# An encoder layer's weight split: row scales moved from the weights to the activations, four row tiles to an instruction

## The chip, the cores and the metric

One core of a Trainium2 chip runs the whole layer. The metric is the device time of the kernel in microseconds (us), the median of several runs. Engines are named as in the profile: PE (TensorE; PEld its weight loads), DVE (VectorE), ACT (ScalarE), POOL (GpSimd), SP (SyncE, which here issues the DMA transfers).

## The reference

One layer over 256 tokens of width 2048, all in fp32. Every sub-layer is wrapped in two root-mean-square norms, one before (with a gain per feature) and one after:

```
def _rmsnorm(x, g):
    return x * rsqrt(mean(x * x, -1) + EPS) * g
def _swiglu(u, w_gate, w_up, w_down):
    return (silu(u @ w_gate) * (u @ w_up)) @ w_down

h = h + 0.5 * _rmsnorm(_swiglu(_rmsnorm(h, ffn1_pre_g), ...), ffn1_post_g)   # D_FF = 5632
h = h + _rmsnorm(_mixer(_rmsnorm(h, mix_pre_g), w_qkv, na_rpb, out_g, w_o), mix_post_g)
h = h + 0.5 * _rmsnorm(_swiglu(_rmsnorm(h, ffn2_pre_g), ...), ffn2_post_g)
g = sigmoid(_rmsnorm(h, ple_pre_g) @ w_ple_gate)
h = h + _rmsnorm(g * (p @ w_ple_proj), ple_post_g)
```

The mixer has 16 heads of 128: 4 with neighbourhood attention, 12 with a mixture of dilated windows. Their outputs are normed per head, multiplied by `out_g` and projected by `w_o`. Five of the gains (the three `pre_g` of the FFNs and the mixer, `ple_pre_g`, `out_g`) multiply the rows of a weight matrix if one wishes: u * g @ w is the same as u @ (g * w).

## The kernel before

**Splitting.** Matmuls run on a rounded fp32 type (`F32R`). To keep precision each factor is split into a high part (a copy into that type) and a low part (the rest), and every product is three matmuls: high by high, low activation by high weight, high activation by low weight. Tokens make two tiles `t` of 128; `NB` = 512 output columns make one block, whose two accumulators (one per token tile) are PSUM tiles of `ps_acc` (4 buffers).

**The weights** stream from HBM in fp32, each used once per token tile. `load_pairs` (L61) fetches up to four row tiles of 128x512 by one DMA on SP (`raw`, 3 buffers) and splits them into pairs: `wh` and `wl` hold two row tiles each and have 7 buffers, 14 row tiles. Where the product has a gain (`g`), each row tile is one ACTIVATE on ACT with the gain as per-partition scale (L79) and one scalar_tensor_tensor on DVE, raw * g - wh (L80). The products without one (down, the embedding's projection) copy and subtract a pair at a time (L74, L75).

**A product** (`product`, L89) goes through its rows in groups of `SUPER` = 8 row tiles: load and split the group, then for both token tiles and all 8 row tiles the three matmuls L114, L115, L116, 48 in all. The very first gate product takes groups of 1, 1, 2, 2, ..., the very first up groups of 4 (L240 to L242), as x and h arrive (`load_x`, L176; `load_h`, L185). Between groups it runs the jobs that were put off (`later`); `mid` is called three row tiles before the end of the last group (L108).

**The activations** are split as they are made, in `transposed_split` (L146): four PE transposes of a 128x512 block into a PSUM tile `tr` (`ps_tr`, 2 buffers), ACT's copy to the high part (L152), DVE's subtract to the low part (L153). It is called for the hidden blocks of the FFNs (`hid`), for the heads' outputs (`on`, L431), and at the end of a stage in `residual` (L198): h += f * r on DVE (L210), then the transposed split of h into `u_h`, `u_l`, for two token tiles and four blocks. The factors r of the norms come from sums of squares on ACT (L144), a reduction on DVE (L137) and two small POOL instructions (L138, L139); they are applied to the products when these are read from PSUM.

**Stages.** First FFN; q, k, v and attention in four rounds of four heads; `w_o` (`mo`); second FFN; the embedding's projection (`pp`) and gate (`pg`). An FFN takes its 11 hidden blocks in groups of 4, 4 and 3 (`FF_GROUPS`): for each block gate and up, then for the group down, whose rows are these blocks' columns. The last hidden block of a group is thus turned just when its down product begins. At the end of a stage `residual` makes the next stage's operand: three transitions, first FFN to q, mixer (`mo`) to second FFN's gate, second FFN to `pg` (with `pp` in between).

**Order.** Each engine runs its instructions in one program order, which the framework's scheduler makes from the code; buffers are handed on by semaphores. An instruction whose operand is late holds up all that stand behind it on its engine.

Of the kernel before, what the change touches and what calls it, by code (L numbers as in the profile page):

```python
# [8 lines left out]
F32 = mybir.dt.float32  # L9
# [19 lines left out]
MID = 3  # L29
BIG = 3.0e38  # L30
# [3 lines left out]
def encoder_layer(ctx: ExitStack, tc: tile.TileContext, a: dict, out: bass.AP):  # L34
# [26 lines left out]
    def load_pairs(w, r0, nk, c0, g):  # L61


        pairs = []
        for k0 in range(0, nk, 4):
            n = min(4, nk - k0)
            raw = wpool.tile([P, 4, NB], F32, name="raw", bufs=3)
            rows_ = w[r0 + k0 * P : r0 + (k0 + n) * P, c0 : c0 + NB]
            raw_loads.append(nc.sync.dma_start(raw[:, :n], rows_.rearrange("(k p) n -> p k n", p=P)))
            for j in range(0, n, 2):  # L70
                wh = wpool.tile([P, 2, NB], F32R, name="wh", bufs=7)
                wl = wpool.tile([P, 2, NB], F32R, name="wl", bufs=7)
                if g is None:
                    nc.scalar.copy(wh, raw[:, j : j + 2])  # L74
                    nc.vector.tensor_tensor(wl, raw[:, j : j + 2], wh.bitcast(F32), op=ALU.subtract)  # L75
                else:
                    for i in range(min(2, n - j)):
                        k = r0 // P + k0 + j + i
                        nc.scalar.activation(wh[:, i], raw[:, j + i], AF.Copy, scale=g[:, k : k + 1])  # L79
                        nc.vector.scalar_tensor_tensor(  # L80
                            wl[:, i], raw[:, j + i], g[:, k : k + 1], wh[:, i].bitcast(F32),
                            op0=ALU.mult, op1=ALU.subtract,
                        )
                pairs.append((wh, wl))
        return pairs
# [3 lines left out]
    def product(  # L89
        acc, lhs, w, r0, c0, g=None, first=True, last=True, steps=None, ahead=None, mid=None, jobs=True  # L90
    ):

        nk = len(lhs)
        s0 = 0  # L100
        for n in steps or [nk % SUPER] * (nk % SUPER > 0) + [SUPER] * (nk // SUPER):
            if ahead is not None:
                ahead(s0)
            pairs = load_pairs(w, r0 + s0 * P, n, c0, g)
            for t in range(NT):
                tok = slice(t * P, (t + 1) * P)
                for k in range(n):
                    if mid is not None and t == NT - 1 and s0 + n == nk and k == n - MID:  # L108
                        mid()
                    wh, wl = pairs[k // 2]  # L110
# [3 lines left out]
                    nc.tensor.matmul(acc[t], xh[:, tok], wh[:, k % 2], start=lead, stop=False)  # L114
                    nc.tensor.matmul(acc[t], xl[:, tok], wh[:, k % 2], start=False, stop=False)  # L115
                    nc.tensor.matmul(acc[t], xh[:, tok], wl[:, k % 2], start=False, stop=tail)  # L116
# [29 lines left out]
    def transposed_split(x, hi, lo, t):  # L146

        tr = ps_tr.tile([P, KB, P], F32, name="tr", tag="tr")
        for k in range(KB):
            nc.tensor.transpose(tr[:, k], x[:, k * P : (k + 1) * P], ident)  # L150
        tok = slice(t * P, (t + 1) * P)
        nc.scalar.copy(hi[:, :, tok], tr)  # L152
        nc.vector.tensor_tensor(lo[:, :, tok], tr, hi[:, :, tok].bitcast(F32), op=ALU.subtract)  # L153
# [22 lines left out]
    def load_x(k):  # L176
        if k % 2:
            return
        hi, lo = (u[:, k % KB : k % KB + 2] for u in x_blocks[k // KB])
        xb = work.tile([P, 2, S], F32, name="xb", tag="hg")  # L180
        nc.sync.dma_start(xb, xT[:, k : k + 2])
        nc.scalar.copy(hi, xb)
        nc.vector.tensor_tensor(lo, xb, hi.bitcast(F32), op=ALU.subtract)
# [14 lines left out]
    def residual(fg, ssf, scale, blocks, rs):  # L198

        blocks += [new_split(acts, "u", D // NB) for _ in range(D // NB)]
        r = []
        for b0 in range(0, D // NB, 2):
            for t in range(NT):
                if b0 == 0:
                    r.append(rsqrt_mean(ssf[t], D, scale))
                for b in range(b0, b0 + 2):
                    cols = slice(b * NB, (b + 1) * NB)
                    nc.vector.scalar_tensor_tensor(  # L210
                        h[:, t, cols], fg[:, t, cols], r[t], h[:, t, cols], op0=ALU.mult, op1=ALU.add
                    )
# [7 lines left out]
    def swiglu(pool, f, ssf, res, blocks, rs, g_pre, w_gate, w_up, w_down, g_post):  # L220
        lhs = rows(blocks)
        f0 = 0
        for gi, ng in enumerate(FF_GROUPS):
            hid = []
            for nb in range(f0, f0 + ng):
# [69 lines left out]
    with ExitStack() as att:  # L295
# [84 lines left out]
        def attend(qT, kT, v, bias, o_split):  # L380

            for t in range(NT):
# [48 lines left out]
                later.append(lambda on=on, t=t: transposed_split(on, *o_split, t))  # L431
# [3 lines left out]
        for g in range(4):  # L435
# [5 lines left out]
            product(acc, lhs, a["w_qkv"], 0, c[0], g=row_g[:, 1])  # L441
            qT = heads_transposed(acc, rq, g > 0, "qT")
            acc = accs("k")
            product(acc, lhs, a["w_qkv"], 0, c[1], g=row_g[:, 1])
            kT = heads_transposed(acc, rs, g > 0, "kT")
            acc = accs("v")
            product(acc, lhs, a["w_qkv"], 0, c[2], g=row_g[:, 1])
# [8 lines left out]
            attend(qT, kT, v, bias, o_split)  # L456
# [7 lines left out]
    res = residual(f, ssf, 1.0, u_blocks, rs)  # L464
# [7 lines left out]
    for b in range(2):  # L472
        acc = accs("mo")
        product(acc, lhs[:early], a["w_o"], 0, b * NB, g=row_g[:, 4], last=False, jobs=b > 0)
        started.append(acc)
    for b in range(D // NB):
# [9 lines left out]
        product(acc, lhs[k0:], a["w_o"], k0 * P, b * NB, g=row_g[:, 4], first=k0 == 0, mid=mid)  # L486
# [9 lines left out]
    with tc.tile_pool(name="ffn2", bufs=2) as pool:  # L496
# [30 lines left out]
    for b in range(D // NB):  # L527
# [3 lines left out]
        product(acc, lhs, a["w_ple_gate"], 0, b * NB, g=row_g[:, 3])  # L531
# [77 lines left out]
```

## Time and profile before

| | us |
|---|---|
| median of 3 runs | 1991.73 (1990.23 to 1991.98) |
| the profiled execution | 1990.87 |
| its span | 1988.8 |
| PE busy in the span | 1969.9 (99%) |
| DVE busy | 1155.9 (58%) |
| ACT busy | 1050.2 (53%) |
| weight loads: 84 to 88 DMAs of 1 MB each for gate, up and down, median time from issue to landing | 5.0 to 5.1 |

The profile is one execution. Its span runs from the first to the last instruction recorded; all starts in the timeline count from the span's start. A row of the groups names line, engine, operation, the tile written and those read, the form, the count, and then busy us, mean ns of one, and the idle time of the engine just before them with what ended it. A row of the timeline begins with start and duration in us; consecutive like instructions are drawn together (x8), and the brackets tell how long the engine stood idle before and what ended that.

### The profile page before, as it was taken

How to read it: one execution, taken by the hardware profiler on the slowest of the kernel's cores; microseconds unless marked ns; L12 is line 12 of the kernel's file. 1: busy time of each engine (PE TensorE's matmuls, PEld its weight loads, DVE VectorE, ACT ScalarE, POOL GpSimd, SP SyncE). 2: the span in 40 equal slices, each digit the busy share in tenths (PEclk: the TensorE clock that was granted, in tenths of full speed). 3: DMA queues.
4: the chain of work that ended last, by engine and by line, in shares of the span. 5: the costliest groups of instructions: out<-in, count | busy, mean ns of one | idle time of the engine just before them, and what ended most of it. 6: DMA issues, size and time to landing. Idle time of an engine off the chain costs nothing.

```text
span 1988.8 us, 23482 instructions
## 1 busy us (share of the span) xinstructions
PE 1969.9 (99%) x8936; PEld 1629.7 (82%) x8936; DVE 1155.9 (58%) x1659; ACT 1050.2 (53%) x1613; POOL 25.4 (1%) x47
## 2 busy tenths in 40 slices
PE   8999999999999999999999999999999999999998
PEld 7888888888888877888888888888888888888886
DVE  5755455655465666566565575654465545565764
ACT  7645455544455455655556564544454534454663
POOL 0000000000000000000000000000000000000000
PEclk9999999999999999999999999999999999999999
DMA  8755555555555557364554555555555555555562
GB/s 302 242 192 187 194 193 189 190 191 188 194 198 183 197 183 224 134 201 138 170 170 168 187 192 200 179 203 175 206 181 200 179 201 184 197 183 203 172 213 102
DMA packets 194561, 377.02 MB, mean 190 GB/s; under 512 B 10768, under 2 KB 13968, under 8 KB 194192
## 3 DMA queue, kind: packets, MB, share of 16 engines
q1 hardware_dynamic: 194448, 375.52, 55.1%
q8 instruction: 70, 1.15, 0.2%
q14 instruction: 43, 0.35, 0.0%
HBM read 373.40 MB, written 2.10 MB: 189 GB/s over the span
## 4 chain that ended last, share of the span: by engine, by line
PE 96%; DMA 1%; DVE 1%; ACT 1%; issue 0%; POOL 0%; SPq 0%; DVEq 0%; POOLq 0%; ACTq 0%
PE down L116 8%; PE down L114 8%; PE down L115 8%; PE up L116 8%; PE up L114 8%; PE up L115 8%; PE gate L116 8%; PE gate L115 8%; PE gate L114 8%; PE tr L150 2%; PE q L116 1%; PE q L115 1%; PE q L114 1%; PE pg L116 1%; PE pg L114 1%; PE k L116 1%
## 5 line engine op out<-in xcount | busy, mean ns | idle before, releaser
L79 ACT ACTIVATE wh<-raw,row_g 128x512 fp32r<-128x512 f32 x1024 | 686.7, 717 | 456.0 <-PE up L115 184.2
L80 DVE SCALAR_TENSOR_TENSOR wl<-raw,row_g,wh 128x512 fp32r<-128x512 f32 x1024 | 708.6, 749 | 335.9 <-ACT wh L79 335.8
L75 DVE TENSOR_TENSOR wl<-raw,wh 128x1024 fp32r<-128x1024 f32 x180 | 220.0, 1224 | 167.5 <-ACT wh L74 153.1
L74 ACT CAST wh<-raw 128x1024 fp32r<-128x1024 f32 x180 | 189.8, 1055 | 213.1 <-PE down L115 168.7
L114 PE MATMUL gate<-wh,u_h 128*128 128x512 f32 x704 | 276.5, 393 | 6.0 <-ACT wh L79 6.0
L116 PE MATMUL gate<-wl,u_h 128*128 128x512 f32 x704 | 275.2, 391 | 0.0
L115 PE MATMUL gate<-wh,u_l 128*128 128x512 f32 x704 | 275.1, 391 | 0.0
L114 PE MATMUL down<-wh,hid_h 128*128 128x512 f32 x704 | 274.5, 390 | 0.0
L116 PE MATMUL down<-wl,hid_h 128*128 128x512 f32 x704 | 274.1, 389 | 0.0
L116 PE MATMUL up<-wl,u_h 128*128 128x512 f32 x704 | 274.0, 389 | 0.1
L114 PE MATMUL up<-wh,u_h 128*128 128x512 f32 x704 | 274.0, 389 | 0.0
L115 PE MATMUL down<-wh,hid_l 128*128 128x512 f32 x704 | 273.9, 389 | 0.0
L115 PE MATMUL up<-wh,u_l 128*128 128x512 f32 x704 | 273.9, 389 | 0.0
L114 PEld LDWEIGHTS gate<-wh,u_h 128*128 128x128 f32 x704 | 132.9, 189 | 32.9 <-ACT wh L79 6.0
L116 PEld LDWEIGHTS gate<-wl,u_h 128*128 128x128 f32 x704 | 132.7, 188 | 27.9 <-DVE wl L80 0.3
L116 PEld LDWEIGHTS up<-wl,u_h 128*128 128x128 f32 x704 | 132.1, 188 | 28.2 <-DVE wl L80 0.5
L115 PEld LDWEIGHTS gate<-wh,u_l 128*128 128x128 f32 x704 | 132.8, 189 | 27.0
L114 PEld LDWEIGHTS up<-wh,u_h 128*128 128x128 f32 x704 | 132.1, 188 | 27.5 <-ACT wh L79 0.3
L115 PEld LDWEIGHTS up<-wh,u_l 128*128 128x128 f32 x704 | 132.1, 188 | 27.4
L115 PEld LDWEIGHTS down<-wh,hid_l 128*128 128x128 f32 x704 | 132.2, 188 | 27.4
L116 PEld LDWEIGHTS down<-wl,hid_h 128*128 128x128 f32 x704 | 132.1, 188 | 27.4
L114 PEld LDWEIGHTS down<-wh,hid_h 128*128 128x128 f32 x704 | 132.2, 188 | 27.0
(122 smaller groups left out, 1813.6 us busy)
## 6 DMA issues: line engine op xcount, KB each, us to landing
raw<-in_ffn_w_up SPq DMA_DIRECT2D x88, 1024.0 KB, 5.1
raw<-in_ffn_w_down SPq DMA_DIRECT2D x88, 1024.0 KB, 5.0
raw<-in_ffn_w_gate SPq DMA_DIRECT2D x84, 1024.0 KB, 5.1
raw<-in_w_qkv SPq DMA_DIRECT2D x48, 1024.0 KB, 5.1
raw<-in_w_o SPq DMA_DIRECT2D x16, 1024.0 KB, 5.0
raw<-in_w_ple_gate SPq DMA_DIRECT2D x16, 1024.0 KB, 5.0
raw<-in_ffn_w_gate SPq DMA_DIRECT2D x7, 512.0 KB, 4.4
xb<-in_xT SPq DMA_DIRECT2D x8, 256.0 KB, 3.2
```

Of the source, the lines that this page charges most:

```text
L74: nc.scalar.copy(wh, raw[:, j : j + 2])
L75: nc.vector.tensor_tensor(wl, raw[:, j : j + 2], wh.bitcast(F32), op=ALU.subtract)
L79: nc.scalar.activation(wh[:, i], raw[:, j + i], AF.Copy, scale=g[:, k : k + 1])
L80: nc.vector.scalar_tensor_tensor(wl[:, i], raw[:, j + i], g[:, k : k + 1], wh[:, i].bitcast(F32), op0=ALU.mult, op1=ALU.subtract,)
L114: nc.tensor.matmul(acc[t], xh[:, tok], wh[:, k % 2], start=lead, stop=False)
L115: nc.tensor.matmul(acc[t], xl[:, tok], wh[:, k % 2], start=False, stop=False)
L116: nc.tensor.matmul(acc[t], xh[:, tok], wl[:, k % 2], start=False, stop=tail)
L150: nc.tensor.transpose(tr[:, k], x[:, k * P : (k + 1) * P], ident)
```

## The change

Weights are no longer scaled. `load_pairs` makes one copy on ACT and one subtract on DVE for all four row tiles of a load (128x2048), into `wh` and `wl` of four row tiles with 3 buffers each (12 row tiles). The gains go into the activations: `transposed_split` gets an optional gain and then multiplies the transposed block by it on DVE (`y_g`, in the work buffers tagged `hg`, of which there are two), between the transposes and ACT's copy; from then on `tr` is free. That is the case for the 24 blocks of the three transitions and the 8 blocks of the heads' outputs; hidden blocks have no gain. `load_x` multiplies each of its 8 blocks the same way (`xg`).

```diff
-    def load_pairs(w, r0, nk, c0, g):
-        pairs = []
-        for k0 in range(0, nk, 4):
-            n = min(4, nk - k0)
-            raw = wpool.tile([P, 4, NB], F32, name="raw", bufs=3)
+    def load_pairs(w, r0, nk, c0):
+        parts = []
+        for k0 in range(0, nk, QUAD):
+            n = min(QUAD, nk - k0)
+            raw = wpool.tile([P, QUAD, NB], F32, name="raw", bufs=3)
...
-            for j in range(0, n, 2):
-                wh = wpool.tile([P, 2, NB], F32R, name="wh", bufs=7)
-                wl = wpool.tile([P, 2, NB], F32R, name="wl", bufs=7)
-                if g is None:
-                    nc.scalar.copy(wh, raw[:, j : j + 2])
-                    nc.vector.tensor_tensor(wl, raw[:, j : j + 2], wh.bitcast(F32), op=ALU.subtract)
-                else:
-                    for i in range(min(2, n - j)):
-                        k = r0 // P + k0 + j + i
-                        nc.scalar.activation(wh[:, i], raw[:, j + i], AF.Copy, scale=g[:, k : k + 1])
-                        nc.vector.scalar_tensor_tensor(
-                            wl[:, i], raw[:, j + i], g[:, k : k + 1], wh[:, i].bitcast(F32),
-                            op0=ALU.mult, op1=ALU.subtract,
-                        )
-                pairs.append((wh, wl))
-        return pairs
+            wh = wpool.tile([P, QUAD, NB], F32R, name="wh", bufs=3)
+            wl = wpool.tile([P, QUAD, NB], F32R, name="wl", bufs=3)
+            nc.scalar.copy(wh[:, :n], raw[:, :n])
+            nc.vector.tensor_tensor(wl[:, :n], raw[:, :n], wh[:, :n].bitcast(F32), op=ALU.subtract)
+            parts += [(wh[:, i], wl[:, i]) for i in range(n)]
+        return parts
...
-    def transposed_split(x, hi, lo, t):
+    def transposed_split(x, hi, lo, t, g=None):
...
+        if g is not None:
+            y = work.tile([P, KB, P], F32, name="y_g", tag="hg")
+            nc.vector.tensor_tensor(y, tr, g.unsqueeze(2).broadcast_to([P, KB, P]), op=ALU.mult)
+            tr = y
         nc.scalar.copy(hi[:, :, tok], tr)
         nc.vector.tensor_tensor(lo[:, :, tok], tr, hi[:, :, tok].bitcast(F32), op=ALU.subtract)
...
-        nc.scalar.copy(hi, xb)
-        nc.vector.tensor_tensor(lo, xb, hi.bitcast(F32), op=ALU.subtract)
+        xg = work.tile([P, 2, S], F32, name="xg", tag="sq")
+        g = row_g[:, 0, k : k + 2]
+        nc.vector.tensor_tensor(xg, xb, g.unsqueeze(2).broadcast_to([P, 2, S]), op=ALU.mult)
+        nc.scalar.copy(hi, xg)
+        nc.vector.tensor_tensor(lo, xg, hi.bitcast(F32), op=ALU.subtract)
...
-                    transposed_split(h[:, t, cols], *blocks[b], t)
+                    transposed_split(h[:, t, cols], *blocks[b], t, g[:, b * KB : (b + 1) * KB])
...
-                later.append(lambda on=on, t=t: transposed_split(on, *o_split, t))
+                later.append(lambda on=on, t=t: transposed_split(on, *o_split, t, g))
```

The calls of `product`, `swiglu`, `residual` and `attend` lose or gain the gain accordingly. The scheduler sets the changed program in another order; a row of the pieces below is the instruction's place on its engine, its line, its operation, the tile written and those read, its form, and how many alike follow. In the changed kernel L73 is the weights' subtract, L145 the multiply `y_g`, L148 the low part of a transposed block, L179 and L181 `xg` and `u_l` of x, L208 the residual's h, L467 the mixer's and L267 and L264 the FFN's f.

DVE at the program's start, before:

```order
1 L183 TENSOR_TENSOR u_l<-xb,u_h 128x512
2 L80 SCALAR_TENSOR_TENSOR wl<-raw,row_g,wh 128x512 x2
3 L183 TENSOR_TENSOR u_l<-xb,u_h 128x512
4 L80 SCALAR_TENSOR_TENSOR wl<-raw,row_g,wh 128x512 x2
5 L183 TENSOR_TENSOR u_l<-xb,u_h 128x512
```

and now:

```order
1 L179 TENSOR_TENSOR xg<-xb,row_g 128x512 x2
2 L181 TENSOR_TENSOR u_l<-xg,u_h 128x512
3 L73 TENSOR_TENSOR wl<-raw,wh 128x512 x2
4 L181 TENSOR_TENSOR u_l<-xg,u_h 128x512
5 L73 TENSOR_TENSOR wl<-raw,wh 128x1024
6 L179 TENSOR_TENSOR xg<-xb,row_g 128x512 x2
```

The gains of the first and the second x block stand ahead of the first block's low part.

DVE where the mixer ends and the second FFN's gate begins (`mo` are the mixer's last accumulators, `ssf` sums for the norm), before:

```order
392 L210 SCALAR_TENSOR_TENSOR h<-f,r,h 128x512 x4
393 L80 SCALAR_TENSOR_TENSOR wl<-raw,row_g,wh 128x512
394 L153 TENSOR_TENSOR u_l<-tr,u_h 128x4x128 x2
395 L80 SCALAR_TENSOR_TENSOR wl<-raw,row_g,wh 128x512 x2
396 L469 TENSOR_TENSOR f<-mo_8710,g_post 128x512
397 L137 TENSOR_REDUCE m<-ssf 128x1
398 L80 SCALAR_TENSOR_TENSOR wl<-raw,row_g,wh 128x512
399 L210 SCALAR_TENSOR_TENSOR h<-f,r,h 128x512 x4
400 L153 TENSOR_TENSOR u_l<-tr,u_h 128x4x128 x2
```

and now:

```order
395 L208 SCALAR_TENSOR_TENSOR h<-f,r,h 128x512 x4
396 L145 TENSOR_TENSOR y_g<-tr,row_g 128x512 x2
397 L73 TENSOR_TENSOR wl<-raw,wh 128x2048
398 L148 TENSOR_TENSOR u_l<-y_g,u_h 128x4x128 x2
399 L467 TENSOR_TENSOR f<-mo_7416,g_post 128x512
400 L127 TENSOR_REDUCE m<-ssf 128x1
401 L73 TENSOR_TENSOR wl<-raw,wh 128x2048
402 L208 SCALAR_TENSOR_TENSOR h<-f,r,h 128x512 x3
403 L145 TENSOR_TENSOR y_g<-tr,row_g 128x512 x2
404 L208 SCALAR_TENSOR_TENSOR h<-f,r,h 128x512
405 L148 TENSOR_TENSOR u_l<-y_g,u_h 128x4x128 x2
```

Between h and the first `u_l` one weight piece of a row tile has become two `y_g` and a piece of four row tiles; ahead of the second token tile's h it is again a piece of four for a piece of one.

DVE where the second FFN ends and the embedding's gate begins, from the second token tile's h on, before:

```order
563 L210 SCALAR_TENSOR_TENSOR h<-f,r,h 128x512 x4
564 L80 SCALAR_TENSOR_TENSOR wl<-raw,row_g,wh 128x512 x5
565 L137 TENSOR_REDUCE m<-ssh 128x1
566 L153 TENSOR_TENSOR u_l<-tr,u_h 128x4x128 x2
567 L137 TENSOR_REDUCE m<-ssh 128x1
568 L80 SCALAR_TENSOR_TENSOR wl<-raw,row_g,wh 128x512
569 L153 TENSOR_TENSOR u_l<-tr,u_h 128x4x128
```

and now:

```order
563 L208 SCALAR_TENSOR_TENSOR h<-f,r,h 128x512 x3
564 L73 TENSOR_TENSOR wl<-raw,wh 128x1024
565 L208 SCALAR_TENSOR_TENSOR h<-f,r,h 128x512
566 L73 TENSOR_TENSOR wl<-raw,wh 128x2048
567 L145 TENSOR_TENSOR y_g<-tr,row_g 128x512 x2
568 L73 TENSOR_TENSOR wl<-raw,wh 128x2048
569 L148 TENSOR_TENSOR u_l<-y_g,u_h 128x4x128 x2
570 L145 TENSOR_TENSOR y_g<-tr,row_g 128x512 x2
571 L127 TENSOR_REDUCE m<-ssh 128x1 x2
572 L73 TENSOR_TENSOR wl<-raw,wh 128x2048
573 L148 TENSOR_TENSOR u_l<-y_g,u_h 128x4x128 x2
```

The first two `u_l`, which stood ahead of this piece before (with the first token tile's h), now come behind it: all eight `y_g` and `u_l` of this transition stand among weight pieces of four row tiles.

More of the change, by code (lines that the diff above doesn't have):

```diff
@@ L240, in swiglu @@
                     steps = [1, 1] + [2] * 7
-                    product(gate, lhs, w_gate, 0, nb * NB, g=g_pre, steps=steps, ahead=load_x)
-                    product(up, lhs, w_up, 0, nb * NB, g=g_pre, steps=[4] * 4, ahead=load_h)
+                    product(gate, lhs, w_gate, 0, nb * NB, steps=steps, ahead=load_x)
+                    product(up, lhs, w_up, 0, nb * NB, steps=[4] * 4, ahead=load_h)
                     rs = [prenorm_factor(t) for t in range(NT)]
@@ L245, in swiglu @@
                 else:
-                    product(gate, lhs, w_gate, 0, nb * NB, g=g_pre)
+                    product(gate, lhs, w_gate, 0, nb * NB)
                     gate_out()
-                    product(up, lhs, w_up, 0, nb * NB, g=g_pre)
+                    product(up, lhs, w_up, 0, nb * NB)
                 split = new_split(pool, "hid", 4)
@@ L283, in encoder_layer @@
         ssf, u_blocks, u_rs = square_sums(), [], []
-        res = residual(f, ssf, 2.0, u_blocks, u_rs)
+        res = residual(f, ssf, 2.0, u_blocks, u_rs, row_g[:, 1])
         swiglu(
-            pool, f, ssf, res, x_blocks, None, row_g[:, 0],
+            pool, f, ssf, res, x_blocks, None,
             a["ffn1_w_gate"], a["ffn1_w_up"], a["ffn1_w_down"], a["ffn1_post_g"],
@@ L440, in encoder_layer @@
             acc = accs("q")
[L441 removed]
+            product(acc, lhs, a["w_qkv"], 0, c[0])
             qT = heads_transposed(acc, rq, g > 0, "qT")
             acc = accs("k")
[L444 removed]
+            product(acc, lhs, a["w_qkv"], 0, c[1])
             kT = heads_transposed(acc, rs, g > 0, "kT")
             acc = accs("v")
[L447 removed]
+            product(acc, lhs, a["w_qkv"], 0, c[2])
             v = attn.tile([P, NT, NB], F32, name="v")
@@ L455, in encoder_layer @@
                 bias = lambda t, hh: dil_bias[:, t]
-            attend(qT, kT, v, bias, o_split)
+            attend(qT, kT, v, bias, o_split, row_g[:, 4, g * KB : (g + 1) * KB])
             o_blocks.append(o_split)
@@ L463, in encoder_layer @@
     ssf, u_blocks, rs = square_sums(), [], []
-    res = residual(f, ssf, 1.0, u_blocks, rs)
+    res = residual(f, ssf, 1.0, u_blocks, rs, row_g[:, 2])
     early = 12
@@ L473, in encoder_layer @@
         acc = accs("mo")
-        product(acc, lhs[:early], a["w_o"], 0, b * NB, g=row_g[:, 4], last=False, jobs=b > 0)
+        product(acc, lhs[:early], a["w_o"], 0, b * NB, last=False, jobs=b > 0)
         started.append(acc)
@@ L485, in encoder_layer @@
         k0 = early if b < 2 else 0
-        product(acc, lhs[k0:], a["w_o"], k0 * P, b * NB, g=row_g[:, 4], first=k0 == 0, mid=mid)
+        product(acc, lhs[k0:], a["w_o"], k0 * P, b * NB, first=k0 == 0, mid=mid)
         mix_out(b, acc, 1, gp)
@@ L530, in encoder_layer @@
         acc = accs("pg")
-        product(acc, lhs, a["w_ple_gate"], 0, b * NB, g=row_g[:, 3])
+        product(acc, lhs, a["w_ple_gate"], 0, b * NB)
         for t in range(NT):
```

23 lines of the change are left out of this document (12 added, 11 removed).

## The prediction

> **What bounds the kernel now.** I read the page first, then the waits of TensorE, then the groups by form, then the timeline round every place where TensorE stands still. First the page of the kernel before: the span, the busy time by engine, and the chain that ended last.
>
> ```profile
> span 1988.8 us, 23482 instructions
> PE 1969.9 (99%) x8936; PEld 1629.7 (82%) x8936; DVE 1155.9 (58%) x1659; ACT 1050.2 (53%) x1613; POOL 25.4 (1%) x47
> PE 96%; DMA 1%; DVE 1%; ACT 1%; issue 0%; POOL 0%; SPq 0%; DVEq 0%; POOLq 0%; ACTq 0%
> ```
>
> TensorE (PE) is busy 1969.9 of 1988.8 us, so all that is not TensorE is 18.9 us. The profiled execution took 1990.87 us, 2.07 outside its span, and lies 0.86 under the median of 1991.73. Next, TensorE's waits (what, total us, times, longest), and its last matmul in the timeline (start, duration).
>
> ```profile
> PE gate L114 <- ACT wh L79: 6.0, 1, 6.0
> PE tr L150 <- DVE h L210: 1.6, 2, 1.0
> PE tr L150 <- PE down L115: 0.7, 1, 0.7
> PE tr L150 <- issue: 0.4, 1, 0.4
> 1978.67 0.39 PE L116 MATMUL pg<-wl,u_h 128*128 128x512 f32 x1
> ```
>
> 6.0 us pass before the first matmul and some 10 after the last one, which the change does not touch. In between only about 2.7 us are listed, all at the transposes where one stage's result becomes the next one's operand. So a change that leaves the matmuls alone can win no more than these 2.7 us and a little of the start; it can lose wherever DVE or ACT become late.
>
> **The split itself.** The groups by form (busy us, mean ns, idle before):
>
> ```profile
> L79 ACT ACTIVATE wh<-raw,row_g 128x512 fp32r<-128x512 f32 x1024 | 686.7, 717 | 456.0 <-PE up L115 184.2 <-PE gate L115 112.3 <-PE k L115 33.4
> L74 ACT CAST wh<-raw 128x1024 fp32r<-128x1024 f32 x180 | 189.8, 1055 | 213.1 <-PE down L115 168.7 <-PE up L115 43.6
> L152 ACT CAST u_h<-tr 128x512 fp32r<-128x512 f32 x24 | 13.9, 591 | 1.5 <-PE tr L150 1.2
> L80 DVE SCALAR_TENSOR_TENSOR wl<-raw,row_g,wh 128x512 fp32r<-128x512 f32 x1024 | 708.6, 749 | 335.9 <-ACT wh L79 335.8
> L75 DVE TENSOR_TENSOR wl<-raw,wh 128x1024 fp32r<-128x1024 f32 x180 | 220.0, 1224 | 167.5 <-ACT wh L74 153.1 <-PE down L115 1.0
> L153 DVE TENSOR_TENSOR u_l<-tr,u_h 128x512 fp32r<-128x512 f32 x24 | 16.0, 686 | 1.1 <-ACT u_h L152 1.1
> ```
>
> A plain instruction over 128x2048 is in no row. From 512 to 1024 columns the subtract grows from 686 to 1224 ns, the copy from 591 to 1055. Going on by the same steps gives 1224+2x538 = 2300 ns and 1055+2x464 = 1983 ns; the upper bound is twice the 1024 row, 2448 and 2110. I take 2.30 and 2.0. The new multiplies (y_g, xg) are 128x512 tensor_tensors: 0.69. The split's DVE time falls from 708.6+220.0 = 928.6 to some 340 quads x 2.30 plus the few short ones, about 800, plus 40 x 0.69 = 28; ACT's from 876.5 to about 690. None of that is on TensorE's path, so it is worth nothing by itself. What matters is that DVE runs in program order, and that the piece behind which a short urgent instruction can stand grows from 0.75 to 2.30 us.
>
> [...]
>
> **The steady state.** Two matmul starts 92 matmuls apart, and the release of weight buffers between them:
>
> ```profile
> 300.06 0.39 PE L116 MATMUL up<-wl,u_h 128*128 128x512 f32 x1
> ...
> 302.30 5.42 ACT L79 ACTIVATE wh<-raw,row_g 128x512 fp32r<-128x512 f32 x8 [4.89 <-PE up L115]
> ...
> 320.92 0.39 PE L115 MATMUL gate<-wh,u_l 128*128 128x512 f32 x1
> ```
>
> 20.86/92 = 0.2267 us a matmul; a group of eight row tiles has 48, 10.88 us. Now three buffers of four row tiles stand where seven of two stood. The second quad of the next group takes the buffer whose last reader is the 35th matmul of this one. From the group's start: freed at 34x0.2267+0.42 = 8.13, copied by 10.1, subtracted by 12.45; its low half is wanted at the 63rd matmul, 14.05. That is 1.6 us of slack (1.3 by the upper bounds), and in the new order nothing else of DVE stands in that stretch. I cost it at nothing; ACT and DVE hide it. A tenth of a microsecond over the slack would be paid in some 176 groups.
>
> **The start.** SP's issue of the second x block, DVE's first u_l, the first matmuls, the second u_h, and later a place in the first up; then the x loads' median landing time in us.
>
> ```profile
> 2.61 0.43 SPq L181 DMA_DIRECT2D xb<-in_xT  x1
> 4.56 0.69 DVE L183 TENSOR_TENSOR u_l<-xb,u_h 128x512 fp32r<-128x512 f32 x1 [4.56 <-ACT u_h L182]
> 6.62 0.63 PE L115 MATMUL gate<-wh,u_l 128*128 128x512 f32 x1
> 7.05 0.63 PE L116 MATMUL gate<-wl,u_h 128*128 128x512 f32 x1
> 7.06 0.62 ACT L182 CAST u_h<-xb 128x512 fp32r<-128x512 f32 x1
> 11.26 0.39 PE L114 MATMUL gate<-wh,u_h 128*128 128x512 f32 x1
> ...
> 46.95 0.40 PE L115 MATMUL up<-wh,u_l 128*128 128x512 f32 x1
> 47.45 0.50 PE L116 MATMUL up<-wl,u_h 128*128 128x512 f32 x1
> xb<-in_xT SPq DMA_DIRECT2D x8, 256.0 KB, 3.2
> ```
>
> In the new order both of DVE's first xg stand ahead of its first u_l. The second waits for the second block, which lands between 3.04+3.2 = 6.2 and 7.06, when its copy began. Two instructions of 0.69 later, at 7.6 to 8.4, the second matmul can go: +1.0 to +1.8, I take 1.6. Near 47 us TensorE already loses 0.27 (0.50 for 0.23), where weight copies come behind the squares of h; a first piece of 2.0 instead of 0.72 adds 1.3. Together +3 (2 to 5).
>
> **Before each down product** (three per FFN, six in all) the last hidden block is turned. Before, at the first of them:
>
> ```profile
> 196.69 1.05 ACT L74 CAST wh<-raw 128x1024 fp32r<-128x1024 f32 x1 [0.30 <-PE down L115]
> 196.72 1.03 PE L150 MATMUL tr<-ident,hm 128*128 128x128 f32 x8
> 198.91 1.28 DVE L153 TENSOR_TENSOR hid_l<-tr,hid_h 128x512 fp32r<-128x512 f32 x2
> ```
>
> Now the copy takes 2.0 (to 198.7), its subtract, still ahead of hid_l, 2.3 (to 201.05), and the first hid_l is there at 201.75. TensorE, through the transposes at 197.6, has 17 matmuls that need none of it, to 201.45. So 0.3 plus a handoff, 0.45 each: +2.7 (1 to 4).
>
> **mixer to second FFN.** DVE's h and u_l of the first token tile, the first gate matmul that reads u_l, and the transposes of the second tile:
>
> ```profile
> 1140.28 2.74 DVE L210 SCALAR_TENSOR_TENSOR h<-f,r,h 128x512 f32<-128x512 f32 x4 [0.96 <-POOL r L139]
> 1143.59 1.29 DVE L153 TENSOR_TENSOR u_l<-tr,u_h 128x512 fp32r<-128x512 f32 x2
> 1144.59 0.39 PE L115 MATMUL gate<-wh,u_l 128*128 128x512 f32 x1
> 1149.15 0.63 PE L150 MATMUL tr<-ident,h 128*128 128x128 f32 x4 [1.00 <-DVE h L210]
> ```
>
> Now DVE has h (to 1143.0), y_g twice (to 1144.4), a quad (to 1146.7), and only then u_l (to 1147.4). The matmul of 1144.59 waits 2.8. A second quad stands ahead of h of the second tile, which moves as far as TensorE does, so the 1.00 stays; later transposes go between more matmuls, which gives back some 0.4. +2.4 (1.5 to 4.5).
>
> **First FFN to q.** The second tile's h on DVE and its transposes:
>
> ```profile
> 743.32 2.08 DVE L210 SCALAR_TENSOR_TENSOR h<-f,r,h 128x512 f32<-128x512 f32 x3 [0.72 <-POOL r L139]
> 744.18 0.63 PE L150 MATMUL tr<-ident,h 128*128 128x128 f32 x4 [0.42 <-issue]
> ```
>
> Two quads, one before the last g_post multiply and one before this h, take the place of pieces of 0.74. Followed through the order, h starts at 746.8 (+3.5), and the four transposes behind it pass through two PSUM buffers, each now freed by y_g, one instruction of 0.69 later. +4.2 (2.5 to 6).
>
> **Second FFN to the gate of the embedding.** DVE's weight subtracts, the transposes, the first u_l of the second pair:
>
> ```profile
> 1885.82 3.40 DVE L80 SCALAR_TENSOR_TENSOR wl<-raw,row_g,wh 128x512 fp32r<-128x512 f32 x5
> 1888.88 1.03 PE L150 MATMUL tr<-ident,h 128*128 128x128 f32 x8
> 1890.21 1.29 DVE L153 TENSOR_TENSOR u_l<-tr,u_h 128x512 fp32r<-128x512 f32 x2 [0.93 <-ACT u_h L152]
> ```
>
> Before, the first tile's u_l were done early; now all y_g come after a quad that ends near 1890.0, the u_l after a second one that ends at 1893.6 (+3.4), and a third stands before the last u_l (+2.3, part of it covered by 19 matmuls). +5.4 (3 to 8).
>
> **Attention.** y_g of the heads runs while TensorE has weight products; I take 0.5 (0 to 2) for quads ahead of the score chain.
>
> **Sum:** 3.0+2.7+2.4+4.2+5.4+0.5 = 18.2. On the profiled execution 2009.1; on the median 2009.9, about 2010. About 0.2% (4 us) is what a measurement of this kernel can tell from no change.
>
> **Rivals.**
> (A) Not slower: TensorE is covered at the three transitions. That asks that the quads ahead of u_l are subtracted in DVE's idle time, in the mixer transition begun before 1142.3. For it: DVE idles 42%. Against it: those quads stand behind h and y_g in the order, and TensorE takes its products in order as well. Only the start and little else would remain, about +3: 1995.
> (B) Faster: the listed 2.7 of waits go, and the start costs nothing, because weights are ready sooner: 1989. The start's order speaks against it.
> (C) The ring stalls: if copy and subtract together take over 1.6 us more than I count, from there on every group pays; 0.3 us over is 176x0.3 = +53: 2063. The 1024 rows speak against it.
> (D) The array's clock. At the start the pitch is 0.43 (6.62 to 7.05) until 11.26, then 0.2267. If a wait of some 3 us, as at the mixer or the embedding transition, brings the slow pitch back for a like 11 matmuls, each costs 11x0.2 = 2.2, three of them 6.6: 2017. No wait of that length stands in this trace between the first matmul and the last, so it is open. [...]
>
> **Chances.** My forecast 0.72, (A) 0.10, (B) 0.03, (C) 0.07, (D) 0.08. The lower ends of the terms sum to +10 (2002), the upper ones to +29 (2021), which hardly come together and take in (D). The range is 1998 to 2021: its low end goes part of the way to (A), and what it leaves out is (A), (B) and (C), 2 in 10. Faster by over 0.2%: 0.03, within: 0.10, slower: 0.87, from (B), (A), and the rest.
>
> **What would show it.** Right: the pitch is 0.2267 in the middle of every product; TensorE's idle is up by some 18 us, in rows that name u_l, hid_l, h or y_g as what it waited for, near 1144 to 1150, 743 to 752 and 1888 to 1896 of the old times; first u_l at 7 to 8 us. The 128x2048 subtract is 2.3 to 2.45 us. Wrong: idle in rows of gate or up that name wl (C), a slow pitch after a wait (D), or waits at the transposes no longer than before (A).

## The result and the profile after

The changed kernel takes 2007.90 us (median, 2007.67 to 2008.13, n = 4) beside 1991.23 for the kernel before: a ratio of 1.0085, 95% interval 1.0071 to 1.0098. It is slower by 16.7 us; 2010 was forecast, 1998 to 2021 the range. The page of the changed kernel, its span and busy times:

```profile
span 2006.1 us, 21223 instructions
PE 1976.7 (99%) x8936; PEld 1631.2 (81%) x8936; DVE 1050.7 (52%) x848; ACT 847.2 (42%) x762; POOL 28.5 (1%) x47
```

DVE has lost 105 us of work and ACT 203, with half the instructions, and the span is 17.3 us longer. TensorE's waits in the same execution (what it was to do, for whom it waited, us in total, times, longest; `tr` are transposes):

```profile
PE gate L104 <- ACT wh L72: 6.0, 1, 6.0
PE tr L141 <- issue: 2.6, 2, 1.8
PE gate L105 <- DVE u_l L148: 2.5, 2, 2.2
PE pg L105 <- DVE u_l L148: 1.9, 1, 1.9
PE gate L105 <- DVE u_l L181: 1.9, 1, 1.9
PE up L106 <- DVE wl L73: 1.6, 1, 1.6
PE tr L141 <- DVE h L208: 1.2, 2, 0.8
PE tr L141 <- DVE y_g L145: 1.1, 2, 0.6
```

Beside the 6.0 at the start, 2.7 us of listed waits have become some 13, of which 8.6 are for an activation that DVE still has to make (u_l, y_g, h); 1.9 of these are at the program's start. The new instructions in the groups by form:

```profile
L72 ACT CAST wh<-raw 128x2048 fp32r<-128x2048 f32 x340 | 650.6, 1914 | 880.2 <-PE up L105 288.3 <-PE down L105 198.5 <-PE gate L105 194.6
L73 DVE TENSOR_TENSOR wl<-raw,wh 128x2048 fp32r<-128x2048 f32 x340 | 778.8, 2291 | 759.2 <-ACT wh L72 759.2
L145 DVE TENSOR_TENSOR y_g<-tr,row_g 128x512 f32<-128x512 f32 x32 | 20.6, 683 | 2.6 <-PE tr L141 2.3 <-PE pp L105 0.3
```

The quad's copy takes 1914 ns and its subtract 2291, where 2.0 and 2.30 us were taken, and y_g 683 (0.69 taken).

**Where the time went.** The weight products are the same 8304 matmuls in nearly the same order in every kernel here, so the start of the n-th one, less its start in the kernel before, is the lag at that place. What the lag grows by at each place is the loss there; in the changed kernel it grows by 0.04 us at most over each gate and up product that is away from the places named. "Start" is up to the end of the first up; "downs" is the sum over the six places where a group's down begins; then the three transitions with the products right behind them, and the attention. The last two columns are the total lag in the profiled execution and the measured difference of the medians, both against the kernel before, in us.

| kernel | start | downs | FFN to q | attention | mixer to FFN | FFN to pg | total lag | measured |
|---|---|---|---|---|---|---|---|---|
| forecast | 3.0 | 2.7 | 4.2 | 0.5 | 2.4 | 5.4 | 18.2 | |
| changed | 3.1 | 1.6 | 4.5 | 0.55 | 2.7 | 4.8 | 17.3 | +16.7 |
| pairs | 1.9 | 0 | 2.8 | 0.1 | 0.9 | 1.2 | 6.9 | +7.0 |
| single row tiles | 1.1 | 0 | 1.6 | 0.5 | 0.5 | 1.9 | 5.5 | +6.9 |
| quads, no gains | 2.3 | 1.5 | 2.8 | 0.2 | 1.5 | 0.2 | 8.4 | +9.0 |
| single row tiles, no gains | 0.7 | 0 | 0.4 | 0.3 | -0.1 | 0.3 | 1.5 | -0.2 |
| own buffers for y_g | 3.8 | 1.6 | 4.2 | 0.2 | 3.3 | 1.6 | 14.6 | +15.4 |
| precedence for the residual | 4.3 | 1.5 | 6.8 | 0.8 | 4.0 | 4.7 | 22.1 | +22.7 |

The lag is that of one execution, up to 1.7 off the difference of the medians; the start alone differs by up to 1.2 between kernels whose order is the same there (3.1, 3.8, 4.3). A difference of a few tenths in a cell is not to be read.

**The mixer's end**, DVE and TensorE in the timeline of the changed kernel:

```profile
1149.24 2.74 DVE L208 SCALAR_TENSOR_TENSOR h<-f,r,h 128x512 f32<-128x512 f32 x4 [0.95 <-POOL r L129]
1151.89 1.28 DVE L145 TENSOR_TENSOR y_g<-tr,row_g 128x512 f32<-128x512 f32 x2
1153.09 2.28 DVE L73 TENSOR_TENSOR wl<-raw,wh 128x2048 fp32r<-128x2048 f32 x1
1155.29 1.28 DVE L148 TENSOR_TENSOR u_l<-y_g,u_h 128x512 fp32r<-128x512 f32 x2
1156.03 0.50 PE L105 MATMUL gate<-wh,u_l 128*128 128x512 f32 x1 [2.25 <-DVE u_l L148]
1161.07 0.63 PE L141 MATMUL tr<-ident,h 128*128 128x128 f32 x4 [0.44 <-DVE h L208]
```

It is the chain of the forecast, row by row: h, two y_g, a quad, and the matmul that wants u_l stands 2.25 us. The second tile's h is then waited for 0.44 instead of 1.00; the forecast had this wait staying at 1.00.

**Before a down**, ACT and DVE at the first of the six:

```profile
199.82 1.91 ACT L72 CAST wh<-raw 128x2048 fp32r<-128x2048 f32 x1 [0.81 <-PE down L105]
...
201.76 2.29 DVE L73 TENSOR_TENSOR wl<-raw,wh 128x2048 fp32r<-128x2048 f32 x1 [0.42 <-ACT wh L72]
203.97 0.68 DVE L148 TENSOR_TENSOR hid_l<-tr,hid_h 128x512 fp32r<-128x512 f32 x1
```

hid_l comes 4.1 us after the transposes began (199.86) instead of 2.2 as before. TensorE loses 0.27 here, and as much at the five others.

**The clock** after the first FFN, in windows of the changed kernel (start:end, length, PE, PEld, DVE, ACT, POOL busy, then the granted TensorE clock, DMA share, GB/s):

```profile
751.00:753.00 2.00, 1.25 (x8) 0.84 (x8) 2.00 (x4) 1.71 (x5) 0.00 (x0) 0.95 1.03 338
753.00:754.00 1.00, 0.82 (x5) 0.82 (x5) 1.00 (x3) 1.00 (x4) 0.00 (x0) 0.50 1.04 403
754.00:755.00 1.00, 1.00 (x6) 0.82 (x5) 1.00 (x3) 0.90 (x2) 0.00 (x0) 0.50 0.95 358
755.00:756.00 1.00, 1.00 (x5) 0.90 (x4) 1.00 (x2) 0.20 (x2) 0.00 (x0) 0.50 0.55 111
756.00:757.00 1.00, 1.00 (x6) 0.77 (x5) 0.97 (x4) 0.78 (x2) 0.07 (x1) 0.88 0.47 160
1907.00:1908.00 1.00, 1.00 (x4) 0.64 (x3) 0.66 (x3) 1.00 (x1) 0.23 (x2) 0.50 0.88 340
1908.00:1909.00 1.00, 1.00 (x6) 1.00 (x5) 0.32 (x1) 1.00 (x2) 0.92 (x3) 0.50 1.05 410
```

For 3.4 us from 752.8, and again from 1906.5, the array had half its clock (0.50); in the kernel before the transitions are at 1.00 throughout. In the second stretch matmuls start 0.43 us apart (1907.06 and 1907.49), at 1.00 they start 0.23 to 0.24 apart (1910.93, 1911.15 and 1911.39). That is less than twice as far, so by estimate a stretch accounts for at most half of its 3.4 us, 1.7, of the loss at each of the two. It probably cost less: over the four executions the mean granted clock was 0.996, 0.996, 0.997 and 0.998, the last by that mean with at least one such stretch fewer, and their times were 2008.13, 2007.77, 2007.67 and 2008.03.

### The profile page after: what moved, and what is told of

Its sections match the earlier page's. It is cut to its first block, busy times and chain, and to the rows that moved or that the text cites. A ratio compares the mean times of both kernels' runs of the same rounds, so it can differ in the third digit from the quotient of the medians.

```text
span 2006.1 us, 21223 instructions
## 1 busy us (share of the span) xinstructions
PE 1976.7 (99%) x8936; PEld 1631.2 (81%) x8936; DVE 1050.7 (52%) x848; ACT 847.2 (42%) x762; POOL 28.5 (1%) x47
## 4 chain that ended last, share of the span: by engine, by line
PE 96%; DVE 2%; DMA 1%; POOL 0%; ACT 0%; issue 0%; SPq 0%; DVEq 0%; POOLq 0%; ACTq 0%
PE up L106 8%; PE up L104 8%; PE up L105 8%; PE down L105 8%; PE down L106 8%; PE down L104 8%; PE gate L105 8%; PE gate L106 8%; PE gate L104 8%; PE tr L141 1%; PE pg L105 1%; PE pg L106 1%; PE pg L104 1%; PE v L105 1%; PE k L104 1%; PE k L105 1%
## 5 line engine op out<-in xcount | busy, mean ns | idle before, releaser
L73 DVE TENSOR_TENSOR wl<-raw,wh 128x2048 fp32r<-128x2048 f32 (+2 forms) x353 | 793.5, 2248 | 762.0 <-ACT wh L72 762.0
L72 ACT CAST wh<-raw 128x2048 fp32r<-128x2048 f32 (+2 forms) x353 | 663.4, 1880 | 890.0 <-PE up L105 288.3
L105 PEld LDWEIGHTS gate<-wh,u_l 128*128 128x128 f32 x704 | 132.6, 188 | 32.3 <-DVE u_l L148 3.0
L230 ACT ACTIVATE sig<-gate,r 128x512 f32<-128x512 f32 x44 | 30.2, 687 | 75.2 <-PE gate L106 74.0
L232 DVE SCALAR_TENSOR_TENSOR gs<-gate,r,sig 128x512 f32<-128x512 f32 x44 | 32.9, 748 | 44.0 <-ACT sig L230 44.0
```

Of the source, the lines that this page charges most:

```text
L72: nc.scalar.copy(wh[:, :n], raw[:, :n])
L73: nc.vector.tensor_tensor(wl[:, :n], raw[:, :n], wh[:, :n].bitcast(F32), op=ALU.subtract)
L105: nc.tensor.matmul(acc[t], xl[:, tok], wh, start=False, stop=False)
L230: nc.scalar.activation(s, gate[t], AF.Sigmoid, scale=rs[t])
L232: nc.vector.scalar_tensor_tensor(y, gate[t], rs[t], s, op0=ALU.mult, op1=ALU.mult)
```

## The experiments

Theory throughout: TensorE loses where a short urgent instruction stands behind a long weight piece on DVE, and where the added multiplies lengthen the chain from h to u_l. Rivals: the added multiplies alone (Y), the shorter ring of weight buffers (R). A difference written with a sign is in us against the kernel before; two numbers in brackets are the 95% interval of the ratio.

**Pairs of row tiles** instead of quads, in buffers as before:

```diff
+            for j in range(0, n, 2):
+                m = min(2, n - j)
+                wh = wpool.tile([P, 2, NB], F32R, name="wh", bufs=7)
+                wl = wpool.tile([P, 2, NB], F32R, name="wl", bufs=7)
+                src = raw[:, j : j + m]
+                nc.scalar.copy(wh[:, :m], src)
+                nc.vector.tensor_tensor(wl[:, :m], src, wh[:, :m].bitcast(F32), op=ALU.subtract)
...
```

> Gains in the activations as in the changed kernel, weights split by plain instructions of two row tiles (128x1024), tiles of two row tiles with 7 buffers. Against the kernel before, the changed kernel lost 3.1 us at the start, 1.65 in the six down products, 4.7, 2.7 and 4.5 at the three transitions and 0.6 in the attention. Theory (half the loss is the length of DVE's weight piece ahead of the short urgent instructions, the rest the added multiplies in the chain): start +2, downs 0, transitions +2.7, +1.7, +3.0, together about +9, 2000 us. Rival Y (the added multiplies alone): only the downs come back, +15, 2006. Rival R (the shorter ring of weight buffers, 12 row tiles for 14): nearly all comes back, 1993.

Measured 1997.62 us, +7.0 (ratio 1.0034, 1.0021 to 1.0047), 2 less than the theory's 9. The downs lose nothing, the mixer's end 0.9 for 2.7. Neither rival alone gives 7.

**One row tile to an instruction**, the same buffers (the copy and the subtract of 128x512 in a loop):

> As the run with pairs, but each copy and subtract takes one row tile (128x512), as long as the pieces before the change. Theory: start +1.7, downs 0, transitions +2, +1.2, +2, together about +7, 1998 us, below the run with pairs. Rival Y: no less than the run with pairs, 2006. Rival R: as the run with pairs, 1993.

Measured 1997.47, +6.9 (1.0021 to 1.0047). The theory's 1998 holds, but not that this kernel is faster than the one with pairs: by the medians that step gives nothing. In the lags it gives 1.4 us of 6.9; the largest difference, 1.3, is between FFN and q, where the pairs' execution had half its clock (0.50 from 744 to 747) and this one had not. 7 us of loss remain that the length of the pieces doesn't explain.

**Quads without the gains:**

```diff
-        if g is not None:
-            y = work.tile([P, KB, P], F32, name="y_g", tag="hg")
-            nc.vector.tensor_tensor(y, tr, ..., op=ALU.mult)
-            tr = y
```

and the same for xg. This kernel leaves the gains out altogether, so it computes another function; only its time is of use.

> The changed kernel with the five row gains left out (no y_g, no xg): four row tiles an instruction, nothing added to the activations' chain. Theory: start +1.4, downs +1.65, transitions +3, +1.4, +3, together about +10.5, 2002 us. Rival Y: +3, 1994. Rival R: no change from the changed kernel, 2008.

Measured 1999.58, +9.0 (1.0031 to 1.0061), for the theory's 10.5: quads alone cost 9, so Y is wrong as an only cause. R says no change from the changed kernel and is wrong too.

**The ring alone**: the instructions of before on tiles of four row tiles with 3 buffers:

```diff
+            wh4 = wpool.tile([P, 4, NB], F32R, name="wh", bufs=3)
+            wl4 = wpool.tile([P, 4, NB], F32R, name="wl", bufs=3)
             for j in range(0, n, 2):
-                wh = wpool.tile([P, 2, NB], F32R, name="wh", bufs=7)
-                wl = wpool.tile([P, 2, NB], F32R, name="wl", bufs=7)
+                wh, wl = wh4[:, j : j + 2], wl4[:, j : j + 2]
```

> The kernel before (gains on the weights, its instructions), but wh and wl tiles hold four row tiles with 3 buffers, so a buffer comes free four row tiles at a time. Theory: +0 to +1, 1991 to 1992 us. Rival R: +10 or more, 2001. Rival Y: as the theory.

Measured 1991.45 beside 1990.60, ratio 1.0005 (0.9996 to 1.0015): no difference that can be told. R falls.

**Neither quads nor gains:**

> One row tile to a plain copy and subtract (as the run with single row tiles), and the five row gains left out: neither large pieces nor added multiplies. Theory (these two make up the whole loss): within 1 us of the kernel before, 1990 to 1991.5 us. Rival S (something else of the change costs too, such as the plain instructions themselves or the new order): +3 or more, 1993.5 us.

Measured 1990.29 beside 1990.46, ratio 0.9999 (0.9990 to 1.0008). This kernel, too, leaves the gains out. It closes the square: quads alone +9.0, multiplies alone +6.9, both +16.7, neither -0.2; that the two add up holds within the intervals, which are some 2.5 us wide each way. Plain instructions in place of scaled ones cost nothing that can be measured.

**Own buffers for y_g**:

```diff
-            y = work.tile([P, KB, P], F32, name="y_g", tag="hg")
+            y = work.tile([P, KB, P], F32, name="y_g", tag="yg", bufs=2)
```

> The changed kernel with buffers of its own for y_g. In the changed kernel y_g shares two work buffers with the split p, which is read until the embedding's projection is done, so at the last transition no y_g can go before that. Theory (that sharing holds the first tile's y_g back): the last transition loses 1 to 1.5 instead of 4.5, 2004.5 us in all. Rival (DVE's weight pieces there hold it back): 4 to 4.5 as before, 2008.

The last transition on DVE in the changed kernel, behind the second tile's h:

```profile
1899.05 2.29 DVE L73 TENSOR_TENSOR wl<-raw,wh 128x2048 fp32r<-128x2048 f32 x1 [0.46 <-ACT wh L72]
1901.65 1.29 DVE L145 TENSOR_TENSOR y_g<-tr,row_g 128x512 f32<-128x512 f32 x2 [0.30 <-PE pp L105]
1902.85 2.28 DVE L73 TENSOR_TENSOR wl<-raw,wh 128x2048 fp32r<-128x2048 f32 x1
1905.05 1.28 DVE L148 TENSOR_TENSOR u_l<-y_g,u_h 128x512 fp32r<-128x512 f32 x2
```

and from the first tile's transposes on, where y_g has buffers of its own:

```profile
1889.87 1.28 DVE L145 TENSOR_TENSOR y_g<-tr,row_g 128x512 f32<-128x512 f32 x2
1891.07 0.74 DVE L208 SCALAR_TENSOR_TENSOR h<-f,r,h 128x512 f32<-128x512 f32 x1
1891.73 0.69 DVE L148 TENSOR_TENSOR u_l<-y_g,u_h 128x512 fp32r<-128x512 f32 x1
```

What released y_g at 1901.65 was a matmul of pp, the last reader of the split p. With its own buffers the first tile's y_g runs 12 us earlier, ahead of the quads, and the transition loses 1.6 instead of 4.8. The 3.2 between them include what the half clock cost there, which struck in the changed kernel and not in this one. Measured 2005.54, +15.4 (1.0061 to 1.0091), 1 above the theory's 2004.5. The forecast had the right place and a wrong reason for it: the quads stood first because y_g could not run yet.

**Precedence** for the residual in the scheduler, on the changed kernel (cut to the lines that matter):

```diff
+                    with tc.high_priority(PRIO):
                         nc.vector.scalar_tensor_tensor(h[:, t, cols], ...)
                         transposed_split(h[:, t, cols], *blocks[b], t, ...)
```

> The changed kernel with the residual's h, y_g, u_h and u_l given precedence over the weights in the scheduler, so that at the mixer's end the first u_l stand ahead of the weight piece of four row tiles instead of behind it. Theory O (the order alone: u_l behind the piece): the wait of 2.25 us for the first u_l there falls to 0.5 and the transition's loss from 2.7 to 0.7, 2006 us in all. Theory B (DVE has that much to do before the second tile's h, wherever the pieces stand): the wait for u_l falls, but the wait for h of the second tile grows by about as much, and the transition still loses 2 to 2.7, 2007.5. The other two transitions change by under 1 in both.

Measured 2012.90, +22.7 (1.0098 to 1.0128): 6 more than the changed kernel. Its waits of TensorE for h, then DVE at the mixer's end, and TensorE's transposes of the second tile there:

```profile
PE tr L142 <- DVE h L210: 4.5, 5, 1.6
```

```profile
1156.72 1.28 DVE L149 TENSOR_TENSOR u_l<-y_g,u_h 128x512 fp32r<-128x512 f32 x2
1157.92 2.28 DVE L74 TENSOR_TENSOR wl<-raw,wh 128x2048 fp32r<-128x2048 f32 x1
...
1160.79 2.28 DVE L74 TENSOR_TENSOR wl<-raw,wh 128x2048 fp32r<-128x2048 f32 x1
1163.79 2.74 DVE L210 SCALAR_TENSOR_TENSOR h<-f,r,h 128x512 f32<-128x512 f32 x4 [0.72 <-POOL r L130]
1164.69 0.63 PE L142 MATMUL tr<-ident,h 128*128 128x128 f32 x4 [1.61 <-DVE h L210]
1166.02 0.63 PE L142 MATMUL tr<-ident,h 128*128 128x128 f32 x4 [0.70 <-DVE h L210]
1167.19 1.97 PE L142 MATMUL tr<-ident,h 128*128 128x128 f32 x8 [0.54 <-DVE y_g L146]
```

u_l is now ahead of the quad, and no matmul waits for it there. But both quads still stand between it and the second tile's h, so the wait moves there, as theory B has it. The loss there also grows, from 2.7 to 4.0, beyond both theories, and two things can have done it: the precedence drew the transposes of that tile together on TensorE as well, ahead of the matmuls that had covered them, and the array had half its clock for 3.4 us from 1166.7 (the last eight transposes took 1.97 us, where eight in a row took 1.29 in the changed kernel's timeline at 1150). No run separates the two. Both theories also had the other transitions changing by under 1, and FFN to q lost 2.3 more; there, too, the transposes stand together, and the cause was not taken apart.

**Single row tiles, own buffers and precedence together:**

> The changed kernel with own buffers for y_g, precedence for the residual, and each copy and subtract over one row tile again (tiles of four row tiles with 3 buffers stay). Theory: what is left is the added multiplies: start +1.2, downs 0, transitions +1.3, +0.3, +0.5, together +3.5, 1994.5 us. Rival Y (the added multiplies are most of the loss): +10 or more, 2001.

Measured 1996.75, +6.6 (1.0022 to 1.0047): between theory and rival, and not to be told from single tiles alone (1997.47). FFN to q still loses 2.1, for the theory's 1.3.

**The kernel before with the precedence:**

> The kernel before with the same precedence for the residual's h, u_h and u_l. Theory: the 1.0 us wait for h at the mixer's end and the 0.42 after the first FFN stay, since DVE's pieces there are short already; 0 to -0.5, 1990 to 1991 us, no difference that can be measured. Rival: the 2.7 us of listed waits go, 1988.

Measured 1993.07 beside 1990.18, ratio 1.0014 (1.0004 to 1.0023): a little slower, which neither of the two had; no version here beats the kernel before.

**Short pieces only where something is urgent** (`fine=True` for the first and last products named below; own buffers for y_g):

> The changed kernel with own buffers for y_g, and weights split one row tile at a time only in the products around the transitions: the first gate and up, the last down of each FFN, the first q, the last of the mixer's output, the second FFN's first gate, pp and the first pg. All the others, some three quarters of the loads, keep pieces of four row tiles. Theory (the large pieces cost only where something short is urgent): start +1.0, downs +1.65, transitions +2, +0.5, +1, attention +0.5, together +6.7, 1997 us. Rival (large pieces or their ring cost throughout): above 2001.

Measured 1999.08, +8.5 (1.0028 to 1.0056), 6.9 less than with own buffers alone, and between theory (+6.7) and rival (above 2001). The mixer's end loses 0.7 and FFN to pg 0.1. But the start loses 2.4 for 1.0, and FFN to q 2.8 for 2, of which some 1.3 stand behind it, in the first k: the first product with quads again.

**And in the first down of each group:**

> As the run with short pieces at the transitions, with short pieces also in the first down product of each group. Theory: the six waits for the last hidden block go, 1.6 us less than that run, 1995.4 us. Rival (those waits come from the transposes and ACT's copy, not from the piece ahead): no less than that run.

Measured 1998.87, the same. The six waits are still 0.26 each; the order tells why, and the run says nothing on the rival. ACT, DVE and the weight load that waits, at the first down:

```profile
197.78 1.91 ACT L75 CAST wh<-raw 128x2048 fp32r<-128x2048 f32 x1 [0.53 <-PE down L108]
199.72 2.29 DVE L76 TENSOR_TENSOR wl<-raw,wh 128x2048 fp32r<-128x2048 f32 x1 [1.51 <-ACT wh L75]
201.92 1.28 DVE L151 TENSOR_TENSOR hid_l<-tr,hid_h 128x512 fp32r<-128x512 f32 x2
202.66 0.19 PEld L108 LDWEIGHTS down<-wh,hid_l 128*128 128x128 f32 x1 [0.37 <-DVE hid_l L151]
```

The piece ahead of hid_l is that of the second down product, which was left a quad. With short pieces everywhere (pairs or single tiles) the six waits are gone; that, and not this run, shows that they come from the piece.

In the same execution the first quad of k; the k product alone adds 2.9 to the lag, of the 4.4 that FFN to q loses here:

```profile
771.91 1.90 ACT L75 CAST wh<-raw 128x2048 fp32r<-128x2048 f32 x1 [5.90 <-DMA raw<-in_w_qkv]
773.86 0.50 PE L107 MATMUL k<-wh,u_h 128*128 128x512 f32 x1 [1.61 <-ACT wh L75]
```

This load landed late (ACT had stood idle for 5.90 us), and the copy of all four row tiles, 1.90 us, came before the first matmul could use any of it. The start loses 1.1 in this execution instead of 2.4, with the same order, and the medians of the two kernels are the same, so these single terms scatter by a microsecond or more.

**The gain inside the split**, in place of y_g (and likewise for xg), on the kernel of the run before:

```diff
+            for k in range(KB):
+                gk = g[:, k : k + 1]
+                nc.scalar.activation(hi[:, k, tok], tr[:, k], AF.Copy, scale=gk)
+                nc.vector.scalar_tensor_tensor(lo[:, k, tok], tr[:, k], gk, hi[:, k, tok]..., ...)
```

> As the run with short pieces at transitions and downs, but the gain enters within the activations' split, without y_g and xg: ACT's copy becomes four activations of 128x128 with the gain as per-partition scale, DVE's subtract four scalar_tensor_tensors (tr * g - high); of x two of 128x256 each. Theory (what is left is one more DVE instruction of 0.69 in the chain): start +0.3, transitions +0.5 to +1 each at most, together +1.5, 1992 us. Rival (four short instructions take DVE and ACT as long as y_g did): as the run before it.

Measured 1999.60, +9.0 (1.0032 to 1.0057); the theory fails by 7.5. The groups by form:

```profile
L150 DVE SCALAR_TENSOR_TENSOR u_l<-tr,row_g,u_h 128x128 fp32r<-128x128 f32 x96 | 30.2, 345 | 5.8 <-ACT u_h L149 4.7
L149 ACT ACTIVATE u_h<-tr,row_g 128x128 fp32r<-128x128 f32 x96 | 32.3, 377 | 12.4 <-DVE u_l L150 6.1 <-PE tr L144 5.8
```

DVE's 30.2 us are for 24 blocks, 1.26 a block, beside 1.30 for y_g and u_l in the changed kernel (20.6 us for 32 and 15.7 for 24), and ACT's part grows from 0.59 to 1.35 (14.2 and 32.3 us for 24). Nothing was saved, and the rival was right by the sum. By places it differs from the run before it: FFN to q loses 3.0 instead of 4.4, the mixer's end 2.8 instead of 0.7.

## Why the prediction was right, step by step

**What bounds the kernel, and the bound on a gain:** as forecast. DVE and ACT lost 308 us of busy time and not one microsecond of it came back. One sign given for it came out smaller: TensorE's time without work grew by 10.5 us (18.9 to 29.4), not 18. The other 6.8 of the span's growth count as busy; at most 3.4 of them are the two stretches at half clock, and the rest was not traced.

**The steady state** was costed at nothing: right. The lag doesn't grow there. The changed kernel's only waits of a product for wl in the list are 1.6 at 34 us and 0.2 in q. Rival (C) did not happen, and the ring alone costs nothing that can be measured.

**The start** came out at 3.1 for 3.0, half of it for the wrong reason. DVE's second xg, held by its load, and the first weights of up, in the changed kernel:

```profile
7.31 0.69 DVE L179 TENSOR_TENSOR xg<-xb,row_g 128x512 f32<-128x512 f32 x1 [2.55 <-DMA xb<-in_xT]
7.92 0.68 DVE L181 TENSOR_TENSOR u_l<-xg,u_h 128x512 fp32r<-128x512 f32 x1
8.66 0.79 PE L105 MATMUL gate<-wh,u_l 128*128 128x512 f32 x1 [1.88 <-DVE u_l L181]
...
31.91 2.29 DVE L73 TENSOR_TENSOR wl<-raw,wh 128x2048 fp32r<-128x2048 f32 x1 [4.61 <-ACT wh L72]
34.25 0.50 PE L106 MATMUL up<-wl,u_h 128*128 128x512 f32 x1 [1.59 <-DVE wl L73]
```

The second matmul went at 8.66 instead of 6.62, 2.0 later (1.6 taken; the x blocks landed after 4.1 us, median, instead of 3.2), and 0.3 of that came back since the fast pitch (0.23 us instead of 0.43) began after 9 matmuls instead of 12. The step that failed: a loss of 1.3 near 47 us, by weight copies behind the squares of h. There the lag shrank by 0.54, since what the kernel before loses at that place is gone. The loss came at 34 us, 1.75, at the first quad of up: ACT's copy of it began at 29.96, when its load had landed, and it had to be copied and subtracted whole before the third matmul could go. With pairs or single tiles this loss is not there. That the sum of the start came out right was luck.

**Before the downs**: 0.27 each for 0.45, 1.6 in all for 2.7. The chain is the one foretold; the size was off.

**Mixer to FFN**: 2.7 for 2.4, the wait for u_l 2.25 for 2.8. Shown by the runs: 1.5 with quads and no gain, 0.5 with the gain and single tiles.

**First FFN to q**: 4.5 for 4.2. The second tile's h started 7.1 us later than in the kernel before (750.44 beside 743.32), of which 3.9 is lag brought along: 3.2 for the 3.5 worked out. But the sum was right without a part of it that the forecast had not counted, up to 1.7 us by half the clock; so the waits themselves may have cost less than worked out. Without a half clock, quads and no gains lose 2.8 here, single tiles with gains 1.6.

**Second FFN to pg**: 4.8 for 5.4, and the reason was wrong. The working followed the order, in which y_g stands behind a quad; it stands there because its two buffers were still held by the split p. Own buffers take away 3.2 of the 4.8, the half clock included, and quads without gains lose only 0.2 here. That the number came out near was luck in part.

**Attention**: 0.55 for 0.5. The kernel of single tiles without gains, which has neither quads nor y_g, shows 0.3 there, so the term is within the scatter and its reason is not shown.

**Rival (D)** had a chance of 0.08 and came in part: a half clock at two of the three transitions, at most 1.7 each for the 2.2 foretold, in or behind waits of 1.82 and 1.92 us. The longer wait of 2.25 was not followed by any, and no run shows what told them apart. Each of the two slow stretches lasted 3.4 us.

**Smaller pieces against large ones:** on the changed kernel, going from quads to single tiles takes 9.8 of 16.7 us away, the two half-clock stretches included, while DVE's busy time grows from 1050.7 to 1145.8 us.

## What to carry to other kernels

With the bounding engine at 99%, the length of an instruction on a half-idle engine (DVE, 52%) counted here by what stood behind it, not by its throughput: the same subtract in pieces of 2.29 us instead of 0.69 cost 9 us in some ten places and nothing that shows in the some 170 groups of matmuls between. The multiplies moved from a stream with slack (weights) into a chain that is waited for (h to u_l) cost time, few as they were: 40 multiplies of 0.69 us cost 6.9 with single tiles, while the same gains on the weights cost nothing that can be measured (-0.2 without them). And an order must be read together with the buffers: an instruction may stand late not because the scheduler put it there but because its buffer has another reader.

## What the runs showed of the hardware that was not expected

The clock fell in or behind short waits. Eight times between the first and the last product, in the profiled executions of four kernels that are otherwise at 1.00 from some 14 us on, the granted TensorE clock went to 0.50 for 3.4 us. In the lists of TensorE's waits of these four, none behind the first matmul is longer than the 2.25 us at the mixer's end. How long TensorE was busy in the 3.41 us ahead of each fall, a stretch as long as the slow one behind it, and in the last row ahead of the end of a wait without a fall (the ends of matmuls are modelled in the profile):

| kernel | the 3.41 us end at, us | TensorE busy in them | clock after it |
|---|---|---|---|
| precedence | 753.66 | 0.94 | 0.50 |
| precedence | 1166.67 | 1.26 | 0.50 |
| changed | 752.82 | 1.33 | 0.50 |
| own buffers | 1155.81 | 1.45 | 0.50 |
| changed | 1906.53 | 1.50 | 0.50 |
| precedence | 1910.78 | 1.50 | 0.50 |
| own buffers | 753.04 | 1.55 | 0.50 |
| pairs | 743.88 | 1.61 | 0.50 |
| changed | 1156.03 | 1.16 | 1.00 |

The wait for u_l at the mixer's end is the same in the changed kernel and with own buffers (2.25 us, from 1153.8 on); with own buffers the clock fell within it, at 1155.81, in the changed kernel it stayed at 1.00. There the 3.41 us up to the end of the wait held 1.16 us of work, less than those ahead of seven of the eight falls. So neither the length of a wait nor the work in the 3.41 us ahead tells, in these traces, where the clock falls; what does was not shown.

At one place a drop cost less than the 1.7 us estimated, since TensorE would have waited anyway. With own buffers the matmuls at the mixer's end fell 1.6 us behind at half clock, and 1.5 of it came back at the second tile's transposes, which wait for h. Of that kernel's four executions the one with a mean clock of 0.999, which by that mean has no such stretch, took 2005.05 us, the three at 0.997 took 2005.45 to 2006.52.
